# A small tile for the sample's queries, an early pool for queries, bias and keys, and four stores for the cached keys

## The chip, the cores and the metric

The kernel runs on one core of a Trainium2 chip. The metric is device time in microseconds (us), from runs of the whole program. The engines are TensorE (PE: matmuls; its weight loads are listed as PEld), VectorE (DVE), ScalarE (ACT), GpSimd (POOL) and SyncE (SP). SP issues every DMA of this kernel, in one queue.

## The reference

One layer of a streaming encoder, on a prompt of 2,048 tokens and a sample of 32 tokens that has a cache of 128 earlier tokens. All arrays are float32.

```
a = rmsnorm(x, g_attn)
q_a, k_a, v_a, q_b, k_b, v_b = split(a @ w_in)          # 1024 -> 6 x 512
# group A, 4 heads: differential attention over all earlier keys
p1, p2 = softmax(q1 k1' / 8 + t5 bias + mask), softmax(q2 k2' / 8 + t5 bias + mask)
o_a = (p1 - lam * p2) v_a                               # then a norm per head
# group B, 8 heads: each 64-token chunk sees itself and the 8 chunks before
o_b = softmax(q k' / 8 + band bias) v_b                 # then a norm over 512
h = x + concat(o_a, o_b) @ w_out
h = h + relu(rmsnorm(h, g_mlp) @ w_up) ** 2 @ w_down
h = h + sigmoid(h @ w_ple_gate) * (p @ w_ple_proj)
y = rmsnorm(h, g_final)
```

The sample's attention sees the cached keys and values and its own. The outputs are `y` for prompt and sample, and the new keys and values.

## The kernel before

**Precision.** Each matmul operand is split into a high and a low part (`split`: ACT copies to the rounded type, POOL or DVE subtracts), and `mm3` (L212) issues three matmuls for each pair: high-high (L216), high-low (L217), low-high (L218). The attention matmuls hold high and low parts side by side in their tiles.

**Stages of `run`.** The tokens are four blocks of 512 (`HALVES` pairs them); the sample's 32 ride in block 3.

1. `prep` transposes and scales `x`; `proj` multiplies it by `w_in`. Queries and keys go to the DRAM arrays `qS` and `kS`, values to `vS`.
2. Long-range (group A) attention, first part: `attn_a` for the query tiles in `JA0` = (0,1), (2,3). A tile is a pair of 128 queries, `j` = 0 to 7; `j` = 8 stands for the sample.
3. The projections of group B, woven with the preparation of blocks 2 and 3; `caches` brings the cached keys and values into `kS` and `vS`.
4. Band (group B) attention, `attn_b`, for `JB`, around the rest of `proj`.
5. Long-range attention, second part: `attn_a` for `JA1` = (4,5), (6,7,8). It stands in the program ahead of `outproj(0)`, `outproj(1)` and the MLP of blocks 0 and 1.
6. `outproj`, `mlp`, `gate` and `final` for blocks 0 and 1, then for blocks 2 and 3 (`mlp7`).

**Who sets the order.** The program is traced as written, and a scheduler (`schedule_with_timeline_sim`) then puts the instructions of each engine into an order of its own, by priorities from the program's order and its estimate of when operands and buffers are ready. So attention matmuls stand between those of projections and MLP in TensorE's queue. Each engine works through its queue strictly in that order.

**Memory.** Tiles come from pools, each a stack entry on the left or right side of SBUF. `pool.tile(..., tag, bufs=n)` takes one of n slots of that tag; a new tile waits until the slot's last user is done. A pool opened where another was closed waits in the same way, tile by tile. `Rings` (L109) deals tiles out to several pools in turn; `Lean` (L119) asks a pool for fewer slots. In `run` the left side holds, after `s12.close()` (L1545), `actq`, later `wk`, `fk`, `oq`, and in the place of `oq` then `hq` and `uq`. The right side holds the band attention's pool `b` until `bx.close()` (L1552), and then `a1` (L1558).

**The lines in question.** `caches` (L525) transposes the cached keys, splits them and stores the four heads of each part with one DMA each. `attn_a` (L573) loads, for each head `g`, the bias (`bias_a`: `ba`, one slot), the keys in tiles of 1,024 columns (`ka`, two slots in the first part, three in the second), for the sample also `ks`, each in two DMAs (high and low part on 64 partitions each); then it calls `attn_a_pair` for each `j`. That (L597) takes a query tile (`q`, two slots, for prompt pairs and sample alike), loads it with `load_q` (two DMAs for a pair, four for the sample), multiplies queries by keys (`s`, L639), adds the bias (L648) or not (L646) while it takes the maximum, exponentiates (L654), combines the two maps (L659, L660), transposes (`tpp`, L698) and multiplies by the values (`o`, L712 to L714). `attn_b_pair` does the same for the band: scores `sb` at L820, transposes `tpb`, output `ob`. `oload` (L925) loads the attention outputs of a block (`oraw`), norms and splits them into `oact`, the operand of `outproj` (`ops`). All DMAs are issued in `dma`, L157.

Of the kernel before, what the change touches and what calls it, by code (L numbers as in the profile page):

```python
# [14 lines left out]
F32R = mybir.dt.float32r  # L15
# [5 lines left out]
P = 128  # L21
D = 1024
SP = 2048
SS = 32
T = SP + SS
PAST = 128
# [47 lines left out]
OW = 1  # L74
# [25 lines left out]
def weave(main, side, step, i=0, n=1):  # L100
    for _ in main:
        if i % step == 0:
            for _ in range(n):
                next(side, None)
        i += 1
    drain(side)
# [37 lines left out]
class Kern:  # L144
# [380 lines left out]
    def caches(self, sg, tp):  # L525
        nc, a = self.nc, self.a
        for grp in range(2):
            nh, dv = (4, 128) if grp == 0 else (8, 64)
            ck = a["cache_a_k"] if grp == 0 else a["cache_b_k"]
            cv = a["cache_a_v"] if grp == 0 else a["cache_b_v"]  # L530
            kn = sg.tile([P, 512], F32, tag="kn", bufs=2, name="ckn")
            self.dma(kn, ck)
            tps = tp.tile([P, 4, P], F32, tag="mm", name="ctp")
            for g in range(4):
                nc.tensor.transpose(tps[:, g], kn[:, P * g : P * g + P], self.ident)
            hi = sg.tile([P, BLK], F32R, tag="qh", bufs=2, name="ckh")[:, :512]
            lo = sg.tile([P, BLK], F32R, tag="ql", bufs=2, name="ckl")[:, :512]
            tf = tps.rearrange("p a b -> p (a b)")
            nc.scalar.activation(hi, tf, AF.Copy)
            nc.vector.tensor_tensor(lo, tf, hi.bitcast(F32), op=ALU.subtract)  # L540
            for i, t in enumerate((hi, lo)):
                for g in range(4):
                    self.dma(
                        self.kS[4 * grp + g, i, :, SP : SP + PAST], t[:, P * g : P * g + P]
                    )
            for c in range(2):
                raw = sg.tile([P, 256], F32, tag="vraw", bufs=2, name="cvr")
                self.dma(raw, cv[:, 256 * c : 256 * c + 256])
                hl = sg.tile([P, nh // 2, 2, dv], F32R, tag="vhl", bufs=2, name="cvhl")
                r3 = raw.rearrange("p (h d) -> p h d", d=dv)  # L550
                self.split(hl[:, :, 0], hl[:, :, 1], r3, "dve", "pool")
                self.dma(
                    self.vS[grp][SP : SP + PAST, 512 * c : 512 * c + 512],
                    hl.rearrange("p a b d -> p (a b d)"),
                )
# [17 lines left out]
    def attn_a(self, js, pool, ps_s, ps_t, ps_o):  # L573
        nc = self.nc
        last = 8 in js
        nk = SP if last else 256 * (js[-1] + 1)
        late = []
        for g in range(4):
            ba = self.bias_a(pool, g)
            kts = [pool.tile([P, 2, 1024], F32R, tag="ka", bufs=2 if self.small else 3, name="ka") for _ in range(0, nk, 1024)]  # L580
            if last:
                ks = pool.tile([P, 2, PAST + SS], F32R, tag="ks", bufs=1, name="ks")
            for hl in range(2):
                src = self.kS[g, hl].rearrange("(m r) c -> r m c", m=2)
                for i, kt in enumerate(kts):
                    c0, n = 1024 * i, min(1024, nk - 1024 * i)
                    self.dma(kt[64 * hl : 64 * hl + 64, :, :n], src[:, :, c0 : c0 + n])
                if last:
                    self.dma(ks[64 * hl : 64 * hl + 64], src[:, :, SP:KC])
            for j in js:  # L590
                self.attn_a_pair(g, j if j < 8 else None, kts if j < 8 else [ks], ba, pool, ps_s, ps_t, ps_o, late)
                if self.small:
                    late.pop(0)()
        while late:
            late.pop(0)()

    def attn_a_pair(self, g, j, ka, ba, pool, ps_s, ps_t, ps_o, late):  # L597
        nc = self.nc
        samp = j is None
        if samp:  # L600
# [2 lines left out]
        else:  # L603
            tiles = [2 * j, 2 * j + 1]
            t0, nq = 256 * j, 256
        q = pool.tile([P, 2, 2, 256], F32R, tag="q", bufs=2, name="q")
        self.load_q(q, g, (0, 1), j)
        ws = []
        for qi, t in enumerate(tiles):
            if samp:  # L610
# [2 lines left out]
            else:  # L613
# [3 lines left out]
                for i in range(nb):  # L617
                    n = min(512, nkeys - 512 * i)
# [11 lines left out]
            c = pool.tile([P, 2], F32, tag="c", bufs=2, name="c")  # L630
# [33 lines left out]
        if samp:  # L664
            kts = [(0, P), (1, SS)]
            vrow = SP
        else:
            kts = [(i, P) for i in range(2 * j + 2)]
            vrow = 0
        o = ps_o.tile([P, 512], F32, tag="o", name="o")  # L670
        for c0 in range(0, len(kts), 4):
# [35 lines left out]
            for x, (i, kn) in enumerate(ch):  # L707
                q0 = 0 if (samp or i <= tiles[0]) else P
                oo = o[:, q0:nq]
                first = c0 + x == 0  # L710
# [214 lines left out]
    def oload(self, b, wk, up, out):  # L925
        nc = self.nc
        n, t0 = BN[b], 512 * b
        if up.whole:
            oact = [up.tile([P, 8, up.aw], F32R, tag="act", name="oact") for _ in range(2)]
            oact = [[t[:, k, :n] for k in range(8)] for t in oact]  # L930
        else:
            oact = [[up.tile([P, up.aw], F32R, tag="u", name="ou")[:, :n] for k in range(8)] for _ in range(2)]
        out[b] = oact
        for k in range(8):
            if k == 4:
                r = wk.tile([P, BLK], F32, tag="r", bufs=2, name="rb")[:, :n]
                self.dma(r, self.rB[:, t0 : t0 + n])
            raw = self.raw_o(wk, k, t0, n)
            if k >= 4:
                nc.vector.scalar_tensor_tensor(  # L940
                    raw, raw, self.g_b[:, k - 4 : k - 3], r, op0=ALU.mult, op1=ALU.mult
                )
            self.split(oact[0][k], oact[1][k], raw, "act", "dve")
            yield
# [496 lines left out]
    def run(self):  # L1441
        tc, nc, a = self.tc, self.nc, self.a
        with ExitStack() as top:

            def opened(stack, name, bufs, space=None, side="left"):
                kw = {} if space is None else {"space": space}
                return stack.enter_context(
                    tc.tile_pool(name=name, bufs=bufs, side=side, reuse_waits="tile", **kw)
                )
# [8 lines left out]
            mm = opened(top, "mm", MM, PSUM)  # L1458
            mmx = ExitStack()
            mz = mm  # L1460
            mm = Rings((mz, "mm"), (mz, "mm"), (opened(mmx, "mmx", 1, PSUM), "mm"))
            tp = mm
            psx = ExitStack()
            ps_s = opened(psx, "pss", 4 - MM, PSUM, "right")
            ps_t = opened(psx, "pst", 2, PSUM, "right")
            ps_o = opened(psx, "pso", 1, PSUM, "right")
# [31 lines left out]
            with ExitStack() as x:  # L1498
                wk = opened(x, "setup", 1, side="right")
# [4 lines left out]
            self.small = True  # L1504
            mark = tc.tile_snap_priority()
            with ExitStack() as x:
                pool = opened(x, "a0", 1, side="right")
                for js in JA0:
                    self.attn_a(js, pool, ps_s, ps_t, ps_o)
            drain(self.proj((0,), 1, acts, sg, mm, tp))  # L1510
# [36 lines left out]
            sq_ = ExitStack()  # L1547
            actq = Sized(opened(sq_, "actq", 2), 512, True)
            oa = {}
# [4 lines left out]
            mm = mz  # L1554
            ps_y = opened(psx, "psy", 1, PSUM, "right")
            sy = Rings((ps_s, "s"), (ps_s, "s"), (ps_y, "s"))
            with ExitStack() as x:
                pool = opened(x, "a1", 1, side="right")  # L1558
                for js in JA1:
                    self.attn_a(js, pool, sy, ps_t, ps_o)  # L1560
            self.nt = 4
            wk = opened(sq_, "wk", 1)
            fk = opened(sq_, "fk", 1)
            self.gfin(fk)
            acc, cn, st = {}, {}, {}
            def norms(b, act, ps):
                self.colnorm(acc[b][0], b, 1.0 / D, wk, ps, "mm", self.rS)
                yield
                yield from self.cnorm(b, wk, act, cn)

            acc = {b: [] for b in range(4)}
            with ExitStack() as x:
                oq = Sized(opened(x, "oq", 2), 512, True)
                weave(self.outproj(0, wk, oa[0], mm, acc[0]), self.oload(1, wk, oq, oa), 1, 0, OW)
                weave(self.outproj(1, wk, oa[1], mm, acc[1]), norms(0, actq, mm), 1, 1)
            hq = opened(sq_, "hq", 1)
            uq = Sized(opened(sq_, "uq", 8), 512)
            up = Sized(opened(top, "uh", 20, side="right"), BLK)
            oxs = ExitStack()
            ox = opened(oxs, "ox", 1, side="right")  # L1580
# [6 lines left out]
            for b in HALVES[0]:  # L1587
# [4 lines left out]
                h = hload(hq, 512, b)  # L1592
# [17 lines left out]
            wk = opened(top, "wk4", 1, side="right")  # L1610
            fk = opened(top, "fk4", 1, side="right")
# [5 lines left out]
            with ExitStack() as x:  # L1617
                act = Sized(opened(x, "acth", 2), BLK, True)
                weave(self.outproj(2, wk, oa[2], md, acc[2]), self.oload(3, wk, act, oa), 1, 0, 2)
                g = self.outproj(3, wk, oa[3], md, acc[3])  # L1620
# [6 lines left out]
                c = self.cparts(2, wk, cs, ops, r2)  # L1627
                weave(g, islice(c, 2), 1)
            hh = [opened(top, f"hh{i}", 1) for i in range(2)]
            h = hload(hh[0], BLK, 0)  # L1630
            g = self.gate(0, h, up, None, md, wk, made[0])
# [7 lines left out]
            h = box[0]  # L1639
# [3 lines left out]
            g = self.gate(2, h, up, None, md, wk)  # L1643
# [8 lines left out]
            h = box[0]  # L1652
# [52 lines left out]
```

## Time and profile before

| | |
|---|---|
| median of 3 runs | 3122.03 us (3116.57 to 3123.8) |
| profiled execution | 3116.1 us |
| its span, first to last instruction | 3114.0 us |
| instructions | 51,781 |
| mean granted TensorE clock | 0.986 |
| DMA traffic | 539.19 MB, mean 173 GB/s |

The profile is of one execution. Rows of a group name line, engine, operation, output<-inputs, shapes and count, then busy time and mean duration, then the idle time of the engine ahead of them and what ended it. A row of the waits says who waited for whom: microseconds in total, times, longest. A row of a timeline begins with start and duration in us; the bracket at its end is the idle time ahead of it and what ended that. A row of the windows gives length, then busy time and count of PE, PEld, DVE, ACT and POOL, the granted TensorE clock, the DMA share and GB/s. A row of the DMA issues ends in count, KB of each, and median us from issue to landing. Matmul ends are modelled, so matmuls overlap in the rows: their rate is read from the distance of their starts.

### The profile page before, as it was taken

The numbers are of one execution on the slowest core, as the hardware profiler recorded it, in microseconds if no ns is written. First come the engines' busy times: TensorE is split into PE (matmuls) and PEld (weight loads), VectorE is DVE, ScalarE is ACT, GpSimd is POOL, SyncE is SP. The second block draws the span as 40 slices with busy tenths as digits, with TensorE's granted clock in tenths as the row PEclk, the third lists the DMA queues.
The fourth block names the chain that finished last, engine by engine and source line by source line (L and its number), as shares of the span: only waits on it lengthen the run. The fifth ranks groups of instructions, "written<-read, shape, count | busy, mean of one in ns | idle before, by whom it ended". The sixth has DMA issues, their size and how long they took to land. (4 is left out here: it accounts for less than half of the span.)

```text
span 3114.0 us, 51781 instructions
## 1 busy us (share of the span) xinstructions
PE 2992.9 (96%) x17801; PEld 2639.7 (85%) x17801; DVE 1815.1 (58%) x4404; ACT 1779.4 (57%) x3446; POOL 1859.1 (60%) x2512
## 2 busy tenths in 40 slices
PE   8998988999999999999999999999899999999998
PEld 7787877999877887788788888779788887999998
DVE  5256574654466554566655654425667884576663
ACT  6256665765666774566655645454655545554545
POOL 2456745423445543665645556677878888767674
PEclk9999999999999999999999999999999999999999
DMA  9797866976788555565665443538434446333231
GB/s 285 261 263 226 243 199 211 269 225 197 213 248 268 154 148 139 151 172 147 192 173 146 126 122 108 162 98 261 154 116 136 139 159 223 117 109 102 89 117 57
DMA packets 523278, 539.19 MB, mean 173 GB/s; under 512 B 38748, under 2 KB 401568, under 8 KB 523016
## 3 DMA queue, kind: packets, MB, share of 16 engines
q1 hardware_dynamic: 523016, 535.89, 57.3%
q8 instruction: 141, 2.31, 0.3%
q14 instruction: 121, 0.99, 0.1%
HBM read 421.97 MB, written 117.75 MB: 173 GB/s over the span
## 5 line engine op out<-in xcount | busy, mean ns | idle before, releaser
L176 POOL TENSOR_TENSOR wl<-wr,wh 128x256 fp32r<-128x256 f32 x648 | 482.3, 776 | 322.6 <-ACT wh L181 271.2
L181 ACT ACTIVATE piece<-wr 128x512 fp32r<-128x512 f32 x406 | 245.8, 625 | 269.2 <-PE ups L217 116.0
L176 POOL TENSOR_TENSOR piece<-wr,piece 128x256 fp32r<-128x256 f32 x404 | 326.5, 834 | 101.9 <-ACT piece L181 80.7
L181 ACT ACTIVATE wh<-wr 128x1024 fp32r<-128x1024 f32 x228 | 240.5, 1056 | 224.7 <-PE ups L217 56.8
L166 POOL TENSOR_TENSOR wl<-wr,wh 128x256 fp32r<-128x256 f32 x264 | 197.2, 777 | 166.9 <-ACT wh L181 162.0
L216 PE MATMUL dps<-uh,piece 128*128 128x272 f32 (+1 forms) x768 | 246.4, 324 | 7.2 <-ACT piece L181 2.9
L166 POOL TENSOR_TENSOR piece<-wr,piece 128x256 fp32r<-128x256 f32 x280 | 234.4, 868 | 27.8 <-ACT piece L181 24.9
L1158 DVE TENSOR_TENSOR h<-h,dps 128x512 f32<-128x512 f32 x256 | 174.2, 683 | 130.1 <-PE dps L218 128.6
L218 PE MATMUL dps<-uh,piece 128*128 128x272 f32 (+1 forms) x768 | 247.1, 324 | 1.3 <-POOL piece L166 1.1
L217 PE MATMUL dps<-ul,piece 128*128 128x272 f32 (+1 forms) x768 | 247.3, 323 | 0.2 <-DVE ul L187 0.2
L216 PE MATMUL ups<-cs,piece 128*128 128x256 f32 (+1 forms) x864 | 245.7, 285 | 1.6 <-DVE r L1217 1.6
L217 PE MATMUL ups<-cs,piece 128*128 128x256 f32 (+1 forms) x864 | 245.7, 285 | 0.0
L218 PE MATMUL ups<-cs,piece 128*128 128x256 f32 (+1 forms) x864 | 245.5, 284 | 0.0
L216 PE MATMUL qps<-aH,wh 128*128 128x512 f32 (+1 forms) x640 | 228.6, 357 | 1.2 <-DVE ql L477 0.9
L217 PE MATMUL qps<-aL,wh 128*128 128x512 f32 (+1 forms) x640 | 227.2, 355 | 0.0
L218 PE MATMUL qps<-aH,wl 128*128 128x512 f32 (+1 forms) x640 | 227.0, 355 | 0.0
L1206 DVE TENSOR_TENSOR h<-h,dps 128x272 f32<-128x272 f32 (+1 forms) x384 | 189.1, 514 | 51.9 <-PE dps L218 51.1
L216 PE MATMUL dps<-uh,wh 128*128 128x512 f32 x512 | 211.6, 413 | 7.0 <-ACT relu L1123 4.4
L654 ACT ACTIVATE e<-e,nm 128x128 f32<-128x128 f32 (+16 forms) x136 | 157.1, 1156 | 97.4 <-DVE nm L652 96.9
L217 PE MATMUL dps<-ul,wh 128*128 128x512 f32 x512 | 203.5, 397 | 0.0
L218 PE MATMUL dps<-uh,wl 128*128 128x512 f32 x512 | 203.1, 397 | 0.0
L216 PE MATMUL ups<-cH,wh 128*128 128x512 f32 x512 | 202.0, 395 | 0.5 <-ACT relu L1123 0.5
(310 smaller groups left out, 9370.5 us busy)
## 6 DMA issues: line engine op xcount, KB each, us to landing
wr<-w_up SPq DMA_DIRECT2D x128, 512.0 KB, 3.9
wr<-w_down SPq DMA_DIRECT2D x128, 512.0 KB, 3.8
wr<-w_in SPq DMA_DIRECT2D x74, 512.0 KB, 5.5
q<-qS SPq DMA_DIRECT2D x128, 256.0 KB, 5.6
v<-vSa SPq DMA_DIRECT2D x64, 512.0 KB, 3.6
ka<-kS SPq DMA_DIRECT2D x32, 512.0 KB, 8.0
wr<-w_out SPq DMA_DIRECT2D x32, 512.0 KB, 5.0
wr<-w_ple_gate SPq DMA_DIRECT2D x32, 512.0 KB, 4.2
```

The lines of the kernel that those rows point to most:

```text
L166: nc.gpsimd.tensor_tensor(out[:, sl], a[:, sl], b[:, sl], op=op)
L176: nc.gpsimd.tensor_tensor(out[:, sl], a[:, sl], b[:, sl], op=op)
L181: nc.scalar.activation(hi, raw, AF.Copy)
L216: nc.tensor.matmul(ps, lh, rh, start=start and i == 0, stop=False)
L217: nc.tensor.matmul(ps, lh, rl, start=False, stop=False)
L218: nc.tensor.matmul(ps, ll, rh, start=False, stop=stop and i == n - 1)
L654: nc.scalar.activation(row, row, AF.Exp, bias=nmx, accum_out=z[:nr, m : m + 1])
L1158: nc.vector.tensor_tensor(hv, hv, ps, op=ALU.add)
L1206: nc.vector.tensor_tensor(hv, hv, ps, op=ALU.add)
```

## The change

- `caches`: the four heads' stores of each part become one DMA with a rearranged access pattern (4 DMAs in all in place of 16, the same bytes).
- `queries` (new) takes the query tile and loads it: for the sample a tile `qs` of 32 columns, one slot, from `attn_a`'s own pool; for prompt pairs a tile `q`, two slots, from `self.qpool`.
- `attn_a` loads the first query tile of a head ahead of its keys, the bias behind them; keys come from `self.kpool`, the bias from `self.qpool`.
- In the first part `qpool` and `kpool` are the part's own pool, as before. In the second part `qpool` is a new pool `ak` on the left side, opened ahead of `a1`; `kpool` deals two of every three key tiles from `ak`'s two slots and one from `a1`.
- `wk`, `fk`, `hq` and `uq` are opened ahead of the second part, in this order; `oq` is gone, and `oload(1)` takes its high parts from `hq` (one tile) and its low parts from `uq` (eight tiles).

```
 caches
-                for g in range(4):
-                    self.dma(
-                        self.kS[4 * grp + g, i, :, SP : SP + PAST], t[:, P * g : P * g + P]
-                    )
+                self.dma(
+                    self.kS[4 * grp : 4 * grp + 4, i, :, SP : SP + PAST].rearrange("g p c -> p g c"),
+                    t.rearrange("p (g c) -> p g c", c=P),
+                )
 attn_a
-            ba = self.bias_a(pool, g)
-            kts = [pool.tile([P, 2, 1024], F32R, tag="ka", bufs=2 if self.small else 3, name="ka") for _ in range(0, nk, 1024)]
+            q = self.queries(g, js[0], pool)
+            kts = [self.kpool.tile([P, 2, 1024], F32R, tag="ka", bufs=2, name="ka") for _ in range(0, nk, 1024)]
...
+            ba = self.bias_a(self.qpool, g)
             for j in js:
-                self.attn_a_pair(g, j if j < 8 else None, kts if j < 8 else [ks], ba, pool, ps_s, ps_t, ps_o, late)
+                self.attn_a_pair(g, j if j < 8 else None, kts if j < 8 else [ks], ba, pool, ps_s, ps_t, ps_o, late, q)
+                q = None
...
+    def queries(self, g, j, pool):
+        if j is None:
+            q = pool.tile([P, 2, 2, SS], F32R, tag="qs", bufs=1, name="qs")
+        else:
+            q = self.qpool.tile([P, 2, 2, 256], F32R, tag="q", bufs=2, name="q")
+        self.load_q(q, g, (0, 1), j)
+        return q
 attn_a_pair
-        q = pool.tile([P, 2, 2, 256], F32R, tag="q", bufs=2, name="q")
-        self.load_q(q, g, (0, 1), j)
+        q = self.queries(g, j, pool) if first is None else first
 oload
+        if isinstance(up, tuple):
+            oact = up[0].tile([P, 8, n], F32R, tag="h", name="oact")
+            oact = [
+                [oact[:, k] for k in range(8)],
+                [up[1].tile([P, up[1].aw], F32R, tag="u", name="ou") for _ in range(8)],
+            ]
 run
-                pool = opened(x, "a0", 1, side="right")
+                self.qpool = self.kpool = pool = opened(x, "a0", 1, side="right")
...
+            wk = opened(sq_, "wk", 1)
+            fk = opened(sq_, "fk", 1)
+            hq = opened(sq_, "hq", 1)
+            uq = Sized(opened(sq_, "uq", 8), 512)
+            self.qpool = opened(sq_, "ak", 1)
             with ExitStack() as x:
                 pool = opened(x, "a1", 1, side="right")
+                self.kpool = Rings((self.qpool, "ka"), (self.qpool, "ka"), (Lean(pool, 1), "ka"))
                 for js in JA1:
                     self.attn_a(js, pool, sy, ps_t, ps_o)
             self.nt = 4
-            wk = opened(sq_, "wk", 1)
-            fk = opened(sq_, "fk", 1)
...
-            with ExitStack() as x:
-                oq = Sized(opened(x, "oq", 2), 512, True)
-                weave(self.outproj(0, wk, oa[0], mm, acc[0]), self.oload(1, wk, oq, oa), 1, 0, OW)
-                weave(self.outproj(1, wk, oa[1], mm, acc[1]), norms(0, actq, mm), 1, 1)
-            hq = opened(sq_, "hq", 1)
-            uq = Sized(opened(sq_, "uq", 8), 512)
+            weave(self.outproj(0, wk, oa[0], mm, acc[0]), self.oload(1, wk, (hq, uq), oa), 1, 0, OW)
+            weave(self.outproj(1, wk, oa[1], mm, acc[1]), norms(0, actq, mm), 1, 1)
```

More of the change, by code (lines that the diff above doesn't have):

```diff
@@ L595, in attn_a, with attn_a_pair @@
             late.pop(0)()
-    def attn_a_pair(self, g, j, ka, ba, pool, ps_s, ps_t, ps_o, late):
+    def queries(self, g, j, pool):
[5 more added lines that the diff above has]
+        return q
+    def attn_a_pair(self, g, j, ka, ba, pool, ps_s, ps_t, ps_o, late, first=None):
         nc = self.nc
@@ L927, in oload @@
         n, t0 = BN[b], 512 * b
-        if up.whole:
+        if isinstance(up, tuple):
[4 more added lines that the diff above has]
+            ]
+        elif up.whole:
             oact = [up.tile([P, 8, up.aw], F32R, tag="act", name="oact") for _ in range(2)]
```

## The prediction

> **What bounds the kernel now.** I read the page first, then the busy time by stretches, then what TensorE waited for, then the timelines at those waits.
>
> ```profile
> span 3114.0 us, 51781 instructions
> PE 2992.9 (96%) x17801; PEld 2639.7 (85%) x17801; DVE 1815.1 (58%) x4404; ACT 1779.4 (57%) x3446; POOL 1859.1 (60%) x2512
> ```
>
> TensorE is the bound; no other engine passes 60%. The change adds no matmul and removes none, so only TensorE's lost time can move: 3114.0 - 2992.9 = 121 us idle, and what is lost while its clock is low. The windows view (length, busy us per engine, then granted clock, DMA share, GB/s) says where:
>
> ```profile
> 140.00:505.00 365.00, 342.07 (x2014) 297.46 (x2014) 214.59 (x641) 217.32 (x495) 227.33 (x326) 0.98 0.77 226
> 505.00:555.00 50.00, 42.06 (x291) 38.81 (x290) 23.86 (x96) 27.76 (x73) 12.59 (x27) 0.86 0.87 252
> 555.00:1220.00 665.00, 644.76 (x3840) 567.67 (x3839) 368.74 (x1244) 445.97 (x917) 294.95 (x447) 0.99 0.71 205
> 1220.00:1940.00 720.00, 699.70 (x3599) 589.91 (x3598) 432.50 (x1029) 419.39 (x648) 414.27 (x573) 0.99 0.54 151
> ```
>
> I count a stretch's loss as idle time plus (1 - clock) x length: 22.9 + 7.3, 7.9 + 7.0, 20.2 + 6.7 and 20.3 + 7.2 us. The second stretch, the start of band attention, loses 14.9 us in 50. The last is the second long-range part under the MLP.
>
> A scheduler orders this program, so an edit deals the order anew. Listings of both programs, in the order in which the scheduler placed all engines' instructions, show the first 942 matmuls (up to the first long-range scores) in the same order, and the last 6,518 (out-projection of block 2 to the end) too. Only the 10,300 between can change their time.
>
> **Cached keys: 16 stores become 4.** The SP queue in its timeline (start, us, what), and TensorE at the same place:
>
> ```profile
> 504.66 1.81 SPq L157 DMA_DIRECT2D kS<-ckh  x4
> 506.56 1.32 SPq L157 DMA_DIRECT2D kS<-ckl  x3
> ...
> 508.94 1.91 SPq L157 DMA_DIRECT2D kS<-ckh  x4
> 511.12 0.79 SPq L157 DMA_DIRECT2D kS<-ckl  x2
> ...
> 512.43 2.46 SPq L157 DMA_DIRECT2D kS<-ckl  x2
> ...
> 515.41 0.42 SPq L157 DMA_DIRECT2D bb<-dbb  x1
> 515.94 1.14 SPq L157 DMA_DIRECT2D kbt<-kS  x2
> 517.43 1.08 SPq L157 DMA_DIRECT2D q<-qS  x2
> ```
>
> ```profile
> 517.50 0.28 PE L217 MATMUL vps<-wl,aH 128*32 128x256 f32 x1
> 517.61 0.28 PE L218 MATMUL vps<-wh,aL 128*32 128x256 f32 x1
> 522.56 0.66 PE L820 MATMUL sb<-kbt,q 128*128 128x128 f32 x2 [4.67 <-DMA q<-qS]
> ```
>
> SP is busy with these stores for 10 us; band attention's first bias, keys and queries stand right behind, and TensorE runs out of value projections at 517.6, as the query load is issued. Twelve stores fewer at 0.45 us (1.81 / 4) free 5.4 us of SP, and up to 2 us more of the last pair's 2.46.
>
> The new listing shows the effect. Before, no matmul stands between head 0's query load and its first score matmul; after, 20 value matmuls do, 2.4 us at the 0.12 us between the two starts above, and 138 matmuls stand behind the last cached-key store. Value and query projections are now also woven between the first heads' scores. The load took 522.56 - 517.43 = 5.1 us, so a wait of up to 5.1 - 2.4 = 2.7 us may stay. Of the stretch's 14.9 us I leave 3 and gain 12. Bounds: gain 6 (the wait goes only by those 2.4 us, half the low clock stays) to 15 (all).
>
> **Queries in a pool that opens early, and a small sample tile.** In part two a head's two prompt pairs and the sample pair shared two query slots, so the next head's first queries waited until the sample pair's score matmuls had freed a slot. TensorE paid:
>
> ```profile
> PE s L639 <- DMA q<-qS: 10.9, 5, 3.8
> ```
>
> ```profile
> 1225.00:1250.00 25.00, 22.56 (x101) 18.63 (x100) 13.74 (x39) 7.50 (x10) 7.66 (x10) 0.93 0.77 185
> 1590.00:1600.00 10.00, 9.29 (x42) 7.42 (x41) 3.43 (x9) 7.62 (x11) 6.48 (x9) 1.00 1.07 244
> 1680.00:1710.00 30.00, 27.29 (x131) 22.38 (x130) 13.39 (x27) 14.55 (x22) 16.40 (x22) 0.94 0.81 203
> 1780.00:1810.00 30.00, 26.20 (x127) 21.69 (x126) 15.85 (x31) 14.61 (x22) 15.40 (x20) 0.94 0.61 152
> ```
>
> Four of the five waits lie here: idle 2.44 + 0.71 + 2.71 + 3.80 = 9.7 us, and 1.8 + 0 + 1.8 + 1.8 = 5.4 us of clock, 15.0 together. One of them:
>
> ```profile
> 1682.94 1.23 SPq L157 DMA_DIRECT2D q<-qS  x2
> ```
>
> ```profile
> 1686.91 0.39 PE L217 MATMUL dps<-ul,wh 128*128 128x512 f32 x1
> 1687.13 0.40 PE L218 MATMUL dps<-uh,wl 128*128 128x512 f32 x1
> 1690.24 1.17 PE L639 MATMUL s<-ka,q 128*128 128x512 f32 x4 [2.71 <-DMA q<-qS]
> ...
> 1692.00 0.63 PE L218 MATMUL dps<-uh,wl 128*128 128x512 f32 x1
> 1692.43 0.63 PE L216 MATMUL dps<-uh,wh 128*128 128x512 f32 x1
> ...
> 1694.89 0.39 PE L216 MATMUL dps<-uh,wh 128*128 128x512 f32 x1
> 1695.12 0.40 PE L217 MATMUL dps<-ul,wh 128*128 128x512 f32 x1
> ```
>
> The queries are issued 4 us before TensorE needs them and take 7. Behind the gap, starts lie 0.43 us apart in place of 0.22, until 1694.9: some 3.6 us at half speed, 1.8 us lost, as the clock column says. The Trainium skill (TensorE: Matmul & The Clock Gate, section HAM oscillation — how this bites in real kernels) would have only idle gaps over about 3.4 us throttle the clock; by it three of the four would cost idle time alone, and this term would be 11.5 us. The measured spacing after a 2.71 us gap decides against it here.
>
> The listings give each first load's lead, in us of matmul work between load and first use (0.23 per 512-wide matmul, 0.12 per 256):
>
> ```
> part two, heads 0 to 3        before                  after
> q, tiles (4,5)                4.1 28.4 29.8 35.7      324 32.9 31.1 32.9
> q, tiles (6,7,sample)         32.9 6.0 1.4 2.7        31.1 41.5 42.0 44.4
> second key tile, (4,5)        5.1 2.4 1.9 1.9         349 5.0 3.3 1.9
> second key tile, (6,7)        3.9 10.0 27.8 6.4       3.9 5.6 26.3 3.6
> ```
>
> All four short query leads are gone; these loads now wait for a pair one earlier. What is late next is the second key tile. Its price:
>
> ```profile
> 1421.79 1.22 SPq L157 DMA_DIRECT2D ka<-kS  x2
> ```
>
> ```profile
> 1424.92 0.55 PE L639 MATMUL s<-ka,q 128*128 128x128 f32 x4
> ```
>
> ```profile
> q<-qS SPq DMA_DIRECT2D x128, 256.0 KB, 5.6
> ka<-kS SPq DMA_DIRECT2D x32, 512.0 KB, 8.0
> ka<-kS SPq DMA_DIRECT2D x16, 256.0 KB, 4.5
> ```
>
> At a listed lead of 1.9 this tile caused no idle time, since SP ran ahead of its place in the listing. The 512 KB ones (3.9, 5.6, 3.6) take 8.0 us in the median; I put 1 us on them, bounds 0 and 8 - 3.9 + 8 - 5.6 + 8 - 3.6 = 11 us. This part gains 14, bounds 4 and 15.
>
> **Loads that are moved.** Four query and four key loads, 4 x 256 + 2 x 512 + 2 x 256 KB = 2.6 MB, now go out early in the out-projection of block 0, where ACT already waits for attention outputs behind SP:
>
> ```profile
> 866.21 0.34 SPq L157 DMA_DIRECT2D oraw<-oT  x1
> ```
>
> ```profile
> 870.40 1.22 PE L216 MATMUL ops<-oact,wh 128*128 128x512 f32 x2 [4.53 <-ACT oact L181]
> ```
>
> That load still stands behind the last key stores, and three of the block's loads had been issued before it, so I leave the wait; the eight stand behind the block's last load. They add 8 x 0.62 (1.23 / 2) = 5 us of SP and, at this stretch's 205 GB/s, 13 us of DMA; weight loads after them have a listed lead of 8.0 us at the least, 13.2 before. I charge 2 us, bounds 0 and 9. `wk`, `fk`, `hq` and `uq` open earlier on the left, in the same sequence, and `oload(1)` writes as many bytes: nothing. The load of the sample queries is four DMAs as before. That attention ends some 20 us of matmul work later costs nothing: more than 100 us of MLP and gate stand between it and the next out-projection.
>
> **Sum.** -12 - 14 + 2 = -24 on the profiled execution's 3116.1 us: 3092. The median of the runs shown, 3122.0, is 5.9 higher, so I predict 3098. The reordered stretches lose another 30.2 + 26.9 + 27.5 - 15.0 = 70 us to chains that I did not cost; new order may shift that by some 8 us either way.
>
> **Rivals.** *The stores' bytes bind, not their issue* (0.13). 16 x 64 KB go out in both. The Trainium skill (DMA: Bandwidth & Descriptors, section Issuing engines are not separate DMA queues) calls the sequencer's time to start a DMA usually small beside the DMA; by it the merge gives nothing. For it: 2.46 us for two stores is not issue alone. Against: ten rows at 0.4 to 0.5 us per store. The 12 us stay: 3110.
>
> *The waits move* (0.11). The second key tile takes over from the queries: 11 us idle and 3 x 1.8 of clock, and the out-projection pays its 9: 25 us come back, 3123. Against: the 1.9 us lead without idle time.
>
> *Slower: the bias comes last* (0.14). The bias load now stands behind the key loads of its head, in the first part too, whose pool is not early, and GpSimd's mask fill waits for it with other work queued behind:
>
> ```profile
> POOL ba L331 <- DMA ba<-dba: 38.0, 14, 5.0
> ```
>
> Score matmuls stop when VectorE, waiting for the bias, leaves their banks full. With four key loads ahead, 4 x 0.62 = 2.5 us later; eight bias loads in part one at 2.5 + 1.8 of clock cost 34 us: -24 + 34 = +10, 3132. It decides when a bias load's lead to its first use is shorter than its 4 to 5 us. Against: the listed leads stay, shortest 2.4 before and after.
>
> **Numbers.** My forecast has 0.62. It and the first rival are faster, 0.75 together; the second is no change, 0.11; the third slower, 0.14. Some 0.2% (6 us) is what a measurement can tell here. All gains whole and uncosted chains 8 us better: -15 - 15 - 8 = -38, 3084. The range runs from there to 3122, which takes in the second rival nearly and leaves out the third.
>
> **What would show it.** Right: four cached-key stores in the SP queue; TensorE's wait for `q` at the first band head under 3 us and the clock there above 0.95; no wait of `s` for `q` after 1200 us; sample loads to `qs`. Wrong: `s` waiting for `ka`, `ops` waiting for `oact` much over 4.5 us, TensorE idle in 140 to 505 above 23 us, or a busy sum that grows.

## The result and the profile after

| kernel | median | runs | ratio to before, 95% interval |
|---|---|---|---|
| before | 3123.6 us | 8 | |
| after | 3107.9 us | 8 | 0.9952 [0.9937, 0.9966] |
| after, in a second session, before 3122.2 | 3109.5 us | 5 | 0.9961 [0.9949, 0.9973] |

The change is worth 13 to 16 us; forecast were 24. One run of the experiment stores16, below, took 3621.6 us at a granted clock of 0.752 and is left out of its figures. The page of the kernel after (span, then busy time and share of each engine):

```profile
span 3107.1 us, 51764 instructions
PE 2994.4 (96%) x17801; PEld 2640.9 (85%) x17801; DVE 1818.1 (59%) x4404; ACT 1781.5 (57%) x3446; POOL 1855.1 (60%) x2512
```

TensorE's busy time is what it was (2992.9 before); its idle time fell from 121 to 113 us. The same four stretches as before (length, busy us per engine, clock, DMA share, GB/s):

```profile
140.00:505.00 365.00, 346.90 (x2074) 304.60 (x2073) 216.52 (x646) 218.47 (x497) 225.46 (x329) 0.98 0.79 234
505.00:555.00 50.00, 47.76 (x371) 45.53 (x371) 27.57 (x101) 31.54 (x80) 24.33 (x42) 1.00 0.93 262
555.00:1220.00 665.00, 633.43 (x3662) 552.80 (x3662) 355.88 (x1206) 435.87 (x888) 281.50 (x430) 0.98 0.72 204
1220.00:1940.00 720.00, 713.34 (x3703) 601.93 (x3702) 447.13 (x1065) 431.63 (x673) 423.81 (x584) 1.00 0.53 151
```

Three of the four are better: idle time 18.1, 2.2 and 6.7 us where it was 22.9, 7.9 and 20.3, with a full clock in the second and fourth. The third, which holds the out-projection of block 0, is worse: 31.6 us idle for 20.2. TensorE's waits (total us, times, longest):

```profile
PE sb L829 <- DVE stb L832: 9.8, 11, 2.6
PE tpb L851 <- DVE pb L860: 6.9, 7, 4.1
...
PE ops L216 <- ACT oact L181: 5.8, 2, 2.9
PE s L648 <- DMA ka<-kS: 5.7, 3, 2.6
PE dps L216 <- ACT relu L1138: 5.4, 3, 4.6
```

No row of `s` for `q` is left (10.9 us before). New are the waits for key tiles; those for VectorE inside the band grew (`sb` from 7.7 us in 4 waits to 9.8 in 11). The four stores and the first band scores, in SP's and TensorE's timelines:

```profile
496.26 0.41 SPq L157 DMA_DIRECT2D kS<-ckh  x1
496.77 0.52 SPq L157 DMA_DIRECT2D kS<-ckl  x1
...
499.39 0.36 SPq L157 DMA_DIRECT2D kS<-ckh  x1
...
500.40 0.43 SPq L157 DMA_DIRECT2D kS<-ckl  x1
...
513.42 1.23 SPq L157 DMA_DIRECT2D q<-qS  x2
```

```profile
519.05 0.69 PE L829 MATMUL sb<-kbt,q 128*128 128x128 f32 x4
```

The load is issued 5.6 us ahead of the scores (5.1 before), and yet no bracket stands at the scores: TensorE does 45 matmuls in between, where before it had 2.

**Loss by place.** Since every kernel here issues the same 17,801 matmuls, each one's start can be set against the matmul work that the listing puts ahead of it (2,892 us in all, at the spacings of the prediction). The difference is the time lost up to there, idle or at a low clock. It can be compared between kernels place by place. The first line is the loss of the kernel before, the others the change against it, in us; columns are stretches of matmul work; before, after and stores16 are means of two profiled executions. 180 to 450 is the first long-range part, 450 to 750 the band and its projections, 750 to 950 the out-projection of block 0 beside the last band heads, 950 to 1200 the road into the second long-range part, 1200 to 1700 its heads, 1700 to 1850 the end of the first MLP.

```
              0-180  -450  -500  -650  -750  -950 -1200 -1500 -1700 -1850  -end   sum
before (loss)  22.3  40.0  15.7   8.3   5.5  24.1  19.3  12.5  13.8   3.5  56.3
after          +0.8  -9.4 -11.6  +4.3  +2.8 +15.2 -11.8  -0.5 -10.0  +6.9  +1.3 -12.1
stores16       +3.2 -10.1 -11.6  +3.8  -3.3 +14.2  -6.9  -0.6 -10.0  +6.3  +1.8 -13.2
rot            -1.1  -9.9 -12.9  +6.1  +4.7 +16.9  -5.8  +7.9  -6.6   0.0  +2.4  +1.7
keys_late      -1.9 -11.1 -11.6  +3.3  +2.8  +7.3  -2.3  +3.5 -10.5  +6.1  -0.7 -15.1
late           -2.2  -9.8 -11.3  +1.5  +4.6  +4.8  -3.0  +2.3 -10.2  +0.1  +3.1 -20.2
qs_first       -2.9 -10.6 -12.0  +4.3  -0.2  +6.0  -1.4  +1.3 -10.2   0.0  +1.7 -24.0
qs_first16     +2.4  -8.7 -10.7  +4.3  -3.3  +2.2  -1.4  +2.1 -10.2  +0.1  +2.8 -20.5
qs_stores4     +3.7  +2.1 -12.2  +4.3  -3.3  +4.1  -4.2  +0.1 -10.0  -0.1  +3.6 -12.0
stores4        -1.3  -2.3 -11.6  +3.1  -3.3  +1.6  -7.1  +3.7  -4.9  +0.1  +0.5 -21.3
qs_only        -0.5  -3.7  +0.5   0.0  -1.8  +3.6  -0.2  -0.4  -8.7  +1.4  -1.2 -11.0
```

The two executions of the kernel before differ by 4.0 us in 750 to 950, by 3.0 in the last column and by at most 1.6 elsewhere, 8.5 in all; those of the kernel after by 4.6 in 650 to 750 and at most 2.7 elsewhere. So a column tells differences of 5 us. The sums do not rank the kernels, since a profiled execution can lie off its kernel's median: that of stores4 (3098.6 us) is its fastest run, 9 us below the median, and those of qs_first16 (3099.6), qs_stores4 (3108.0) and rot (3121.7) lie 10, 8 and 7 us above theirs.

### The profile page after: what moved, and what is told of

It reads as the page before. It is cut to its first block, busy times and chain, and to the rows that moved or that the text cites. A ratio compares the mean times of both kernels' runs of the same rounds, so it can differ in the third digit from the quotient of the medians.

```text
span 3107.1 us, 51764 instructions
## 1 busy us (share of the span) xinstructions
PE 2994.4 (96%) x17801; PEld 2640.9 (85%) x17801; DVE 1818.1 (59%) x4404; ACT 1781.5 (57%) x3446; POOL 1855.1 (60%) x2512
## 5 line engine op out<-in xcount | busy, mean ns | idle before, releaser
L218 PE MATMUL ups<-cH,wl 128*128 128x512 f32 x512 | 202.1, 395 | 0.0
```

The lines of the kernel that those rows point to most:

```text
L218: nc.tensor.matmul(ps, ll, rh, start=False, stop=stop and i == n - 1)
```

## The experiments

The medians of the kernel before in the four sessions were 3120.3, 3122.2, 3121.7 and 3121.8 us.

**The parts of the change, one at a time.**

*stores4*: the kernel before with four stores.

```
-                for g in range(4):
-                    self.dma(self.kS[4 * grp + g, i, ...], t[:, P * g : P * g + P])
+                self.dma(self.kS[4 * grp : 4 * grp + 4, i, ...].rearrange(...), t.rearrange(...))
```

> The kernel before with the four stores alone. Kernels before and after are 3123.6 and 3107.9 us. Theory A (the sum of the prediction with two terms of another size: stores -12 to -19, queries -15 to -22, early loads and the early score block in the out-projection of block 0 +15 to +22, a later end of attention, which the listing shows with the four stores too, +8): the gain at the band start, 8 lost where the MLP of blocks 0 and 1 ends, the short query leads of the second long-range part still paid: 3112 to 3120. Theory B (the out-projection lost time to the new order as such, not to the early loads): that loss is here too, 3127 to 3135. Theory C (the stores' bytes bind, not their issue): no gain at the band start, 3122 to 3132.

Measured: 3107.2 us, 0.9958 [0.9942, 0.9974]. Better than theory A, and the place table says why: -11.6 at the band start as expected, and no loss in the out-projection (+1.6) nor at the MLP's end (+0.1). Theories B and C fall: this new order does not slow the out-projection, and the band start gains. The listing lets attention end as late as in the kernel after (after 1,797 us of matmul work, 1,775 before), and it costs nothing here.

*qs_only*: the kernel before with the small sample tile.

```
-        q = pool.tile([P, 2, 2, 256], F32R, tag="q", bufs=2, name="q")
+        if samp and not self.small:
+            q = pool.tile([P, 2, 2, SS], F32R, tag="qs", bufs=1, name="qs")
+        else:
+            q = pool.tile([P, 2, 2, 256], F32R, tag="q", bufs=2, name="q")
```

> The kernel before with the small sample tile alone: 16 stores, no early pool, and in the listing no matmul between the first band queries and the first scores, as before. Theory E: the 12 us at the band start are lost again, the query waits after the first head of the second part are gone (9 us): 3107 to 3114. Rival: the second part's gain needs the early pool: 3116 to 3123. Rival: the small tile carries the whole gain of its version with four stores: 3097 to 3103.

Measured: 3109.3 us, ratio 0.9971 [0.996, 0.9982], as theory E has it; both rivals fall. Of the waits of `s` for `q`, the first head's is left, and the band start is as before, with its stall:

```profile
PE s L642 <- DMA q<-qS: 2.3, 1, 2.3
```

```profile
519.05 3.01 PE L823 MATMUL sb<-kbt,q 128*128 128x128 f32 x8 [4.59 <-DMA q<-qS]
```

The later heads gain 8.7 us with no early pool.

*qs_stores4*: both together.

> The kernel before with the four stores and the small sample tile in its own slot, no early pool, bias ahead of the keys, keys in three slots of the part's pool. Theory A: the gains of stores and queries without the early loads in the out-projection: -19 - 18 + 8, 3090 to 3100, faster than the kernel after. Theory B: the out-projection loss stays, 3106 to 3114. Theory D (the early pool carries the query gain, the small tile alone does little): TensorE still waits for q at the heads of the second part, 3108 to 3118.

Measured: 3099.8 us, 0.9933 [0.9916, 0.995], as theory A has it: -12.2 at the band start, -10.0 at the later heads, +4.1 in the out-projection. Theories B and D fall.

**Is it the stores or the order?** *stores16* is the kernel after with 16 stores; it ran twice, the second time beside the kernel after.

> The kernel after with 16 stores again. Theory A: SP is busy with the stores for 10 us again, TensorE waits over 3 us for the first band queries: 3120 to 3127. Theory C (bytes bind, not issue), or the new order alone gave the gain at the band start: 3106 to 3110.

> The kernel after with 16 stores, beside the kernel after on one chip. Theory E (what counts at the band start is how much matmul work the order puts between the first loads and the first scores; the merged stores count only through the order): within 4 us of the kernel after, or faster by what its other order saves, 3096 to 3110. Theory A (SP's issue time of the 12 stores): 6 to 12 us slower than the kernel after, 3112 to 3120.

> The kernel after once more, beside the next three on one chip: 3104 to 3110 if the kernel before is near 3122; a second profiled execution shows which of its waits come back in the same place (the 4.6 us for the squared activations at the end of the first MLP, the 2.6 us for the early key load in the out-projection of block 0).

Measured: 0.9934 [0.992, 0.9949], then 0.9945 [0.9932, 0.9958] beside 0.9961 [0.9949, 0.9973] of the kernel after. Sixteen stores are no slower; the first of the two medians, 3097.6 us, lies below the ranges given for that run. The waits of the kernel after come back in its second execution, at the end of the first MLP and in the early score block; one of `s` for `q` lies in the first long-range part, ahead of 250 us, and none in the second:

```profile
PE dps L216 <- ACT relu L1138: 5.8, 3, 5.2
...
PE s L648 <- DMA ka<-kS: 2.6, 1, 2.6
...
PE s L648 <- DMA q<-qS: 1.8, 1, 1.8
```

SP's timeline and TensorE's of stores16:

```profile
498.31 1.87 SPq L157 DMA_DIRECT2D kS<-ckh  x4
500.29 1.33 SPq L157 DMA_DIRECT2D kS<-ckl  x3
...
502.67 1.84 SPq L157 DMA_DIRECT2D kS<-ckh  x4
504.72 1.74 SPq L157 DMA_DIRECT2D kS<-ckl  x4
...
515.45 1.23 SPq L157 DMA_DIRECT2D q<-qS  x2
```

```profile
521.05 0.62 PE L829 MATMUL sb<-kbt,q 128*128 128x128 f32 x4
```

SP spends its 7 us on the stores, but here the last of them ends 9 us ahead of the query load (2.5 us before), and 47 matmuls run between load and first score (20 in the listing); no bracket stands there. Theories A and C fall, theory E stands.

**Is it the early pool?** *late*: the kernel after with everything from the second part's own pool.

```
-            self.qpool = opened(sq_, "ak", 1)
...
-                self.kpool = Rings((self.qpool, "ka"), (self.qpool, "ka"), (Lean(pool, 1), "ka"))
+                self.qpool = pool
+                self.kpool = Rings((pool, "ka"), (pool, "ka"), (Lean(pool, 1), "kc"))
```

> The kernel after without the early pool: queries, bias and keys come from the second part's own pool, so none of their loads stands in the out-projection of block 0. Theory A: the loss there goes, and the first head of the part pays up to one load's wait: 3086 to 3098. Theory B: the loss stays, since it comes with the new order: 3104 to 3112. Theory D (the early pool earns its price at the first head): 3108 to 3116.

Measured: 3100.5 us, 0.9939 [0.9921, 0.9956], +4.8 in the out-projection for the kernel after's +15.2, and -3.0 for -11.8 on the road into the second part: theory A in its sign, not in its size.

*keys_late*: queries and bias early, the keys (`kpool` as in late) not.

> The kernel after with the keys from the second part's own pool: only queries and bias are loaded early, no score block stands in the out-projection of block 0. Theory F (the early key loads and the score block that follows them make the out-projection's loss): between 700 and 900 us of matmul work it loses 9 us less than the kernel after: 3094 to 3102. Rival (the early pool's mere order makes it): as the kernel after, 3104 to 3110.

Measured: 3102.6 us, 0.9941 [0.9929, 0.9954], just above theory F's range and below its rival's. With the four query loads early and the four key loads not, the out-projection loses 7.3 us for the kernel after's 15.2.

*rot* takes only the score block out of the out-projection, by dealing the key slots in another turn.

```
-                self.kpool = Rings((self.qpool, "ka"), (self.qpool, "ka"), (Lean(pool, 1), "ka"))
+                self.kpool = Rings((Lean(pool, 1), "ka"), (self.qpool, "ka"), (self.qpool, "ka"))
```

> The kernel after with the three key slots dealt in another turn, so that head 0's first key tile comes from the second part's own pool; queries, bias, the second key tile and 1.5 MB of early loads stay early, but no score block stands in the out-projection of block 0. Theory F (the early score block, which waits for its key tile in the out-projection, makes the 7 to 9 us that the kernel after loses between 750 and 800 us of matmul work): these go, 3098 to 3104. Rival G (the early loads' traffic makes them): they stay, 3106 to 3112. On either, the first head of the second part waits for its first key tile at most 4 us.

Measured: 3114.7 us, 0.9981 [0.9967, 0.9994], slower than either theory said. With no score block there and as many bytes of early loads (four of queries, four of keys), the out-projection still loses 16.9: theory F falls, rival G stands. The +7.9 at 1200 to 1500 was not followed up.

How the early loads cost is in the timelines. SP in the kernel after, then in qs_first (below), which has none of them at this place:

```profile
866.47 1.26 SPq L157 DMA_DIRECT2D q<-qS  x2
867.83 1.22 SPq L157 DMA_DIRECT2D ka<-kS  x2
...
869.74 1.48 SPq L157 DMA_DIRECT2D ka<-kS  x2
871.27 0.59 SPq L157 DMA_DIRECT2D ba<-dba  x1
871.90 1.43 SPq L157 DMA_DIRECT2D q<-qS  x2
...
883.26 0.32 SPq L157 DMA_DIRECT2D hd<-xT  x1
```

```profile
863.28 2.27 SPq L157 DMA_DIRECT2D hd<-xT  x1
...
871.26 0.40 SPq L157 DMA_DIRECT2D hd<-xT  x1
...
876.64 0.40 SPq L157 DMA_DIRECT2D hd<-xT  x1
```

`hd` is the residual that VectorE adds to each output unit of the out-projection before its PSUM bank is free (L980). In qs_first three of these loads go out in 14 us; in the kernel after the next one waits until 883.3, behind the early loads and what queued up there. SP issues the early loads in 7 us, but then it also waits for some of them to land before it goes on. Its waits in the kernel after from 866 to 884 us begin with

```profile
SPq L157 <- DMA ka<-kS: 6.0, 4, 1.9
```

(6.2 us in the second execution, 5.1 in rot), and in qs_first it waits there for no load at all. VectorE then TensorE, in rot, where no score block confuses the picture:

```profile
884.53 0.69 DVE L187 TENSOR_TENSOR ou<-oraw,oact 128x512 fp32r<-128x512 f32 x1 [7.16 <-DMA hd<-xT]
885.15 0.68 DVE L980 TENSOR_TENSOR hd<-hd,ops 128x512 f32<-128x512 f32 x1
```

```profile
885.88 0.80 PE L216 MATMUL ops<-oact,wh 128*128 128x512 f32 x1 [4.82 <-DVE hd L980]
```

And the stretch 860 to 890 us in the windows of after, rot and qs_first, in this order:

```profile
860.00:890.00 30.00, 25.00 (x117) 19.98 (x116) 14.52 (x46) 15.02 (x29) 7.81 (x14) 0.94 0.97 237
```

```profile
860.00:890.00 30.00, 24.57 (x114) 20.08 (x113) 14.06 (x48) 17.89 (x34) 11.11 (x19) 0.90 0.97 257
```

```profile
860.00:890.00 30.00, 30.00 (x150) 25.40 (x150) 14.10 (x45) 21.77 (x39) 21.08 (x32) 1.00 0.86 255
```

TensorE gets 117 and 114 matmuls done where qs_first does 150; the difference, at some 0.23 us each, is some 8 us. In the kernel after it waits 2.54 us for the early key tile and then 0.96 us for `hd`, and VectorE waits 8.11 us for `hd`. (The kernel before does 119 here too, with its own 4.53 us wait for `oact` in the stretch; with it the place table compares, not this window.)

*before_again* gives the scatter of executions used above.

> The kernel before in a second profiled execution: near 3121 us. Wherever its loss in a stretch differs by more than 2 us from the first profile's, a difference of the same size between kernels is one of executions and not of the order.

Measured: 3124.6 us.

**The parts that pay, without the others.** *qs_first16* is qs_only with `attn_a` and `queries` as in the kernel after (a head's first queries ahead of its keys, the bias behind them), all tiles from the part's own pool, 16 stores; *qs_first* is the same with four stores.

```
-            ba = self.bias_a(pool, g)
+            q = self.queries(g, js[0], pool)
...
+            ba = self.bias_a(pool, g)
```

> The kernel before with the small sample tile and each head's first queries loaded ahead of its keys, the bias behind them: 16 stores, no early pool. In the listing 20 matmuls then stand between the first band queries and the first band scores, as in the kernel after. Theory E (order, not SP's issue time): the whole band-start gain (12 us), the later heads' (9 us), and the stall of 4.3 us at the end of the first long-range part goes: 3096 to 3103, with no part of the four stores and the early pool. Theory A (the stores' issue): 3108 to 3115. Theory D (the early pool is needed): 3104 to 3110.

> The same with four stores: small sample tile, each head's first queries ahead of its keys, the bias behind them, no early pool. The listing of the second long-range part and the leads at the band start are those of its version with 16 stores (0.9904 of the kernel before, 3089.5 us). Theory E (the merge is worth nothing by itself): within 0.3% of that, 3083 to 3100. Theory A (SP's issue time of 12 stores is worth 6 us or more): under 3083.

Measured: 3089.5 us, 0.9904 [0.9884, 0.9925], and 3095.8 us, 0.9922 [0.9908, 0.9935]. Theory E again: the band start gains 10.7 with 16 stores and 12.0 with four. Both are faster than the kernel after; their own two intervals overlap. The change without the early pool is the best version seen, with or without the merged stores.

## Why the prediction was right, and where it was not

The sign and the range held; the median came out 10 us above 3098. By the prediction's own steps:

**Cached keys, -12.** The size was right (-11.6 in 450 to 500, first query wait 4.67 us to none, clock 0.86 to 1.00), and so was the reading of the listing: the gain comes where matmuls stand between load and scores. The cause that the step gave was not needed for it. It took the stores' time on SP as what kept the load back; stores16 and qs_first16 gain as much with 16 stores, and qs_only, with 3 matmuls between load and scores, still pays 4.59 us. The merge is one of two edits that change the order at this place; loading queries ahead of keys is the other. Whether four stores would help in the old order was not tried, since no version came out in that order. The prediction's first rival had the merge give nothing. Where the order has matmuls behind the load it gave nothing, but the bytes were not the reason: the 12 us that the rival left at this place did go, and its 3110 lies 2 us from the median by luck. The Trainium skill (DMA: Bandwidth & Descriptors, section Issuing engines are not separate DMA queues), which calls the time to start a DMA usually small beside the DMA, fits the stores here: 12 more at 0.45 us of SP each cost nothing that shows. The step also kept the gain whole: in every kernel with the new order at the band start, 1.5 to 6.1 us come back in 500 to 650, where band scores and transposes wait for VectorE (`sb` 9.8 us in 11 waits, 7.7 in 4 before).

**Queries, -14.** The waits that this term priced went, and at its size: -10.0 us at the later heads, and at the first head the 4.2 us (2.44 idle, 1.8 of clock) of the prediction's row. The later heads' gain comes with the small tile alone (-8.7 in qs_only, -6.6 in rot, -10.0 to -10.5 in the seven others; stores4, without it, has -4.9). The first head's wait does not need the early pool: in late, without it, `s` waits once for queries in the whole program, for 0.7 us, and in qs_first not at all in the second part.

The other 7.6 of the 11.8 us gained in 950 to 1200 are no query waits, and no term held them. The kernel before has two more stalls on this road, one of 2.01 us for `e` and one for the MLP's `relu`; both are gone in the kernel after. In late and qs_first a wait for `relu` of 6.16 and 6.43 us stands here. TensorE before, then TensorE, ACT and SP in late:

```profile
1296.57 0.80 PE L216 MATMUL dps<-uh,wh 128*128 128x512 f32 x1 [4.01 <-ACT relu L1123]
```

```profile
1267.53 0.80 PE L216 MATMUL dps<-uh,wh 128*128 128x512 f32 x1 [6.16 <-ACT relu L1138]
```

```profile
1264.70 1.06 ACT L181 ACTIVATE wh<-wr 128x1024 fp32r<-128x1024 f32 x1 [9.48 <-DMA wr<-w_down]
```

```profile
1237.98 1.29 SPq L157 DMA_DIRECT2D q<-qS  x2
...
1260.91 0.38 SPq L157 DMA_DIRECT2D wr<-w_down  x1
```

From 1238 to 1258 us SP is busy with the loads of the part's first pairs, and an MLP weight load stands behind them. So here, too, a burst of loads is paid for by the stage that runs beside it, and the early pool takes part of the burst away. What that is worth is not sharp: 950 to 1200 gains 11.8, 6.9 and 5.8 us in after, stores16 and rot, and 0.2 to 4.2, in the mean 2.0, in the five small-tile kernels without the pool, so 4 to 10 us. But stores4, with neither pool nor tile, gains 7.1 by its order alone.

The 1 us put on the second key tile is about right: the waits for key tiles are 5.7 us in 3 and, in the second execution, 2.6 in 1, and 2.5 of them each time are the early score block's.

**Loads that are moved, +2, bounds 0 to 9.** This is the step that failed: 750 to 950 costs 15.2 us more than before. Six kernels without early loads cost 1.6 to 6.0 there, 3.7 in the mean, so some 11 us are the loads', for the 2 that were charged. The step looked at the activations and weights of the out-projection, and did not look for its residual loads: `hd` stands behind the eight, in SP's queue and behind their 2.6 MB, and SP waits 6.0 us for key tiles to land before it issues it. What the pool gains on the road to the first head, 4 to 10 us, it pays here.

**"Attention ends later costs nothing."** The stretch 1700 to 1850 costs 6.9 us, but the later end is not the reason: stores4 ends as late, qs_first later still, at no cost. ACT's queue has a conversion of the next out-projection's weights ahead of the last `relu`. The kernel after, then stores4:

```profile
1974.77 0.63 ACT L181 ACTIVATE piece<-wr 128x512 fp32r<-128x512 f32 x1 [6.58 <-DMA wr<-w_out]
1975.30 1.04 ACT L181 ACTIVATE wh<-wr 128x1024 fp32r<-128x1024 f32 x1
1976.25 0.58 ACT L1138 ACTIVATE relu<-ups 128x512 f32<-128x512 f32 x1
```

```profile
1969.11 0.58 ACT L1123 ACTIVATE relu<-ups 128x512 f32<-128x512 f32 x1
1971.14 0.63 ACT L181 ACTIVATE piece<-wr 128x512 fp32r<-128x512 f32 x1 [1.46 <-DMA wr<-w_out]
```

With the `relu` behind the conversion, TensorE waits 4.6 us (the row of `dps` above). It happens in after, stores16 and keys_late and not in rot, which also opens the pool early; what tips the order is open.

**The slower rival: bias comes last.** Its mechanism took place and its price did not. GpSimd's wait for the bias grew from 38.0 us to

```profile
POOL ba L331 <- DMA ba<-dba: 51.4, 14, 9.1
```

and yet the first long-range part, where it was to cost 34 us, loses 9.4 less. All seven kernels with queries ahead of keys and the bias behind gain 8.7 to 11.1 us there, the three others between 3.7 gained and 2.1 lost. The longest stall that goes is this one of the kernel before, which is in none of the seven and takes 3.3 to 4.6 us in the three others:

```profile
430.74 0.58 PE L712 MATMUL o<-pH,v 128*128 128x256 f32 x1 [4.34 <-ACT pH L705]
```

Why the new sequence of loads removes it was not tried. No step of the prediction had this gain; it was in the 70 us of chains that were not costed, where 8 us either way were allowed.

Against the 24 us of the sum, the place table has for the kernel after: -11.6 + 4.3 for the first term, -14.2 for the second, +15.2 for the third; -9.4, -7.6 and +6.9 that no step had, and +4.4 for the rest: -12 us. That the forecast came within 10 us is in part luck: misses of 5 to 13 us, on both sides, offset each other.

## What to carry to other kernels

Where a scheduler orders the program, cost an edit by the order it brings, and ask in the experiment whether the order without the edit does the same: here 16 stores did as well as 4 wherever the order had matmuls between the query load and the scores. A burst of loads is paid for by the small loads of the running stage that stand behind it on the queue, so list every load of the stage that it enters, the residuals too, before calling it covered, and ask what it holds up where it is now. Split a change into its parts even when the whole is faster: here the small tile and the earlier queries gave more than the whole.

## What the hardware showed beyond expectation

A short gap costs more than its length. In the kernel after the windows row of 880 to 890 us,

```profile
880.00:890.00 10.00, 6.71 (x28) 5.62 (x29) 1.89 (x4) 2.41 (x5) 0.14 (x1) 0.83 1.09 299
```

has a granted clock of 0.83, and the longest idle gap there is 2.54 us (the wait for the early key tile, which began at 879.8). Behind it, at 884.4 to 885.3, matmul starts lie 0.43 us apart, for 0.23 ahead of it. By the rule of the Trainium skill (TensorE: Matmul & The Clock Gate, section HAM oscillation — how this bites in real kernels) only gaps over some 3.4 us are to be avoided; here, as in the prediction's row of 2.71 us, the clock is low behind a shorter one.

Loads issued together land late: the two 512 KB key loads among the eight that SP issues within 7 us took 12.5 us in the median, for 7.0 over the whole program (DMA views of after from 866 to 895 us, and of its page):

```profile
ka<-kS SPq DMA_DIRECT2D x2, 512.0 KB, 12.5
```

```profile
ka<-kS SPq DMA_DIRECT2D x32, 512.0 KB, 7.0
```
